# A mixture-of-experts stage whose small products stand in one block for two experts, with TensorE's order fixed to that of the weight loads

## The chip, the cores and the metric

The kernel runs on 1 core of one Trainium2 chip. The metric is the device time of one execution in microseconds, the median of several runs; times of one profiled execution are read from its trace. Engines are PE (TensorE), DVE (VectorE), ACT (ScalarE), POOL (GpSimd) and SP (SyncE), whose queue starts the loads of weights.

## What is computed

A first block of attention, a bidirectional state-space mixer and MLPs on 256 tokens of 1024 numbers is followed by a second block of two layers; each has a token mixer and a mixture of 32 experts. All weights and activations are fp32. Cut to what matters:

```python
for l in range(2):
    mod = silu(c) @ ada_w[l] + ada_b[l]
    sh1, sc1, gt1, sh2, sc2, gt2 = split(mod, 6)
    h = modulate(rms_norm(x, norm1_g[l]), sh1, sc1)
    x = x + gt1 * token_mixer(h, ...)
    h = modulate(rms_norm(x, norm2_g[l]), sh2, sc2)
    x = x + gt2 * hier_moe(h, ...)
return rms_norm(x, final_g)

# hier_moe: the best of 4 groups, then 2 of its 8 experts for a token
hid = silu(xb @ w1[e]) * (xb @ w3[e])      # xb: the tokens of expert e; w1, w3: 1024 x 512
y   = (hid @ w2[e]) * weight               # w2: 512 x 1024; summed over the token's experts
```

## The kernel before

Every expert's 6 MB of weights are loaded whatever the routing. `moe_layer` gives each expert 64 slots and takes the experts in 16 pairs `n`; four experts share a group `G` of gathered tokens. These are its steps:

- `gather(G, d, d + 1)` (L1687) picks the tokens of four experts for 128 of the 1024 numbers: four products with the one-hot tile `OH`, one PSUM tile `pb` (two buffers), one eviction to `XT`. Eight of them make a group. `slot_weights` (L1668) and `oht` (L1679) are eight tiny products and four transposes for a group.
- `up(e, half)` (L1706) multiplies expert `e`'s 64 slots with half of w1 and w3: 8 products for w1 (`o` = 0, output partitions 0 to 63) and 8 for w3 (`o` = 1, partitions 64 to 127) in both halves together, each 64x512, into one PSUM tile `acc` (four buffers). After the second half ACT evicts it as `H` (L1722).
- `act(e)` (L1724) transposes `H` in four products into a `pb` tile and forms silu(a) * b as `aT`.
- `down(n, half)` (L1736) multiplies both experts of a pair (`o` = 0 and 1) with w2: 16 products 64x512 for both halves. `gains` evicts the result, weighted and split in two, as `Y`.
- `scatter(G, t, c)` (L1778) adds the results of four experts to the tokens: four products with `OHT`; four calls make a group. `last` (L1788) does it for the last four experts, straight into the layer's end.
- `general` (L1877) is a branch for a routing in which an expert has more tokens than slots. It is not taken here, but each engine reads a number and jumps over it (L1883).

**Loads.** The class `Stream` cuts the weights into jobs of 1 MB, in the order in which `up` and `down` want them: `up(2n)`, `down(n - 1)`, `up(2n + 1)`; 192 jobs a layer, 4 for an `up` and 4 for the `down` of a pair. A job goes into one of 5 tiles `raw` or one of 7 pairs of half tiles `pre`, a ring of 12 MB. SP's queue (L91) issues a load once the products that read the tile's last contents are done. Before a stage of experts begins, 17 jobs are on their way: 12 in the ring and 5 in tiles that are otherwise free at that time.

**Order on PE.** The code is compiled by a scheduler that reorders instructions within an engine by its own costs, unless `tc.issue_after(i)` says that what is written under it comes behind instruction `i`; this sets an order, it is no wait. Before, `slot_weights`, `gather`, `scatter`, `oht` and `add_x` are appended to a list, and `unit()` takes one step from that list after every two `kk` of `up` and every `f` of `down`. PE's order is otherwise free:

```python
            def unit():
                if todo:
                    todo.pop(0)()
```

Of the kernel before, what the change touches and what calls it, by code (L numbers as in the profile page):

```python
# [1580 lines left out]
def moe_layer(K, l):  # L1581
    nc, tc, I, ws = K.nc, K.tc, K.I, K.ws
    with ExitStack() as ctx:
# [67 lines left out]
        with tc.tile_pool(name="moef", bufs=1, reuse_waits="tile") as q:  # L1651
# [15 lines left out]
            def slot_weights(G):  # L1667

                P = K.pb([128, 2, 2])
                for j in range(2):  # L1670
                    for t in range(2):
                        oh = f32(XT[G][0])[:, t, 2 * j:2 * j + 2].rearrange("p e s -> p (e s)")
                        nc.tensor.matmul(P[:, j], oh, W[:, t, 4 * G + 2 * j:4 * G + 2 * j + 2], start=(t == 0), stop=(t == 1))
                for o in range(2):
                    ps = slice(64 * o, 64 * o + 64)
                    nc.scalar.activation(wcol[ps, 2 * G:2 * G + 2], P[ps, :, o], AF.Copy)

            def oht(G):
                OHT[G] = qr[0].tile([128, 2, 256], FR, name="OHT", tag="OHT", bufs=1)  # L1679
                PT = K.pb([128, 2, 2, 128])  # L1680
                for j in range(2):
                    for t in range(2):
                        oh = f32(XT[G][0])[:, t, 2 * j:2 * j + 2].rearrange("p e s -> p (e s)")
                        nc.tensor.transpose(PT[:, j, t], oh, K.ident)
                nc.scalar.activation(OHT[G], PT.rearrange("p j t l -> p j (t l)"), AF.Copy)

            def gather(G, d0, d1):  # L1687
                OH, xt = XT[G]
                for d in range(d0, d1):
                    P = K.pb([128, 4, 64])  # L1690
                    ds = slice(d * 128, d * 128 + 128)
                    for i, (h, t) in enumerate(((h2h, 0), (h2h, 1), (h2l, 0), (h2l, 1))):
                        nc.tensor.matmul(P.rearrange("p e s -> p (e s)"), h[:, t, ds], OH[:, t].rearrange("p e s -> p (e s)"),  # L1693
                                         start=(i == 0), stop=(i == 3))
# [6 lines left out]
            def unit():  # L1701
                if todo:
                    todo.pop(0)()

            def up(e, half):

                G, i = divmod(e, 4)
                if half == 0:
                    H[e] = K.acc()
                P = H[e]  # L1710
                hs = ws.get(4)
                for u in range(2):
                    for kk in range(2):
                        k = half * 4 + u * 2 + kk
                        for o in range(2):
                            nc.tensor.matmul(P[64 * o:64 * o + 64], XT[G][1][k][:, i], hs[2 * o + u].raw[:, kk],  # L1716
                                             start=(k == 0), stop=(k == 7))
                    unit()
                ws.done(4)
                if half:  # L1720
                    H[e] = q.tile([128, 512], F32, name="H", tag="H", bufs=3)
                    nc.scalar.activation(H[e], P, AF.Copy)  # L1722

            def act(e):  # L1724
                PT = K.pb([128, 4, 2, 64])
                for f in range(4):
                    nc.tensor.transpose(PT[:, f].rearrange("p o s -> p (o s)"), H[e][:, f * 128:f * 128 + 128], K.ident)  # L1727
                del H[e]
                s = q.tile([128, 4, 64], F32, name="s1", tag="s1", bufs=2)
                i = nc.scalar.activation(s, PT[:, :, 0], AF.Silu)  # L1730
                aT[e] = q.tile([128, 4, 64], F32, name="aT", tag="aT", bufs=4)
                j = nc.vector.tensor_tensor(aT[e], s, PT[:, :, 1], OP.mult)  # L1732
                K.ah = i.ins, j.ins

            def down(n, half):
# [4 lines left out]
                for u in range(2):  # L1740
                    f = half * 2 + u
                    for c in range(2):
                        cs = slice(c * 512, c * 512 + 512)
                        for o in range(2):
                            nc.tensor.matmul(PY[c][64 * o:64 * o + 64], aT[2 * n + o][:, f], hs[2 * o + u].raw[:, 0, cs],  # L1745
                                             start=(f == 0), stop=(f == 3))
                    unit()
                ws.done(4)

            def gains(j):  # L1750
# [22 lines left out]
            def scatter_pair(P, j, t, c, start, stop):  # L1773
                ts, cs = slice(t * 128, t * 128 + 128), slice(c * 512, c * 512 + 512)
                for i, y in enumerate(Y[j]):
                    nc.tensor.matmul(P, OHT[j // 2][:, j % 2, ts], y[:, cs], start=start and i == 0, stop=stop and i == 1)

            def scatter(G, t, c):  # L1778
                cs = slice(c * 512, c * 512 + 512)
# [37 lines left out]
            slot_weights(0)  # L1817
            for n in range(16):
                G, i = divmod(n, 2)
                if i == 0 and G:  # L1820
                    later(slot_weights, G)
                if i == 1 and G < 7:
                    later(gather_prep, G + 1)
                    for d in range(8):
                        later(gather, G + 1, d, d + 1)
                if n == 15:
                    for t in range(2):
                        for c in range(2):
                            later(add_x, t, c, out[t][:, c * 512:c * 512 + 512])
                up(2 * n, 0)  # L1830
                if n:
                    act(2 * n - 1)
                up(2 * n, 1)
                if n:
                    down(n - 1, 0)
                    act(2 * n)
                    down(n - 1, 1)
                    if n == 1:
                        K.actx.close()
                        qr.append(rctx.enter_context(tc.tile_pool(name="moer", bufs=1, side="right", reuse_waits="tile")))  # L1840
                        out += K.tail(F32)
                        later(oht, 0)
                    gains(n - 1)
                if i == 0 and G:
                    for t in range(2):
                        for c in range(2):
                            later(scatter, G - 1, t, c)
                    later(oht, G)
# [194 lines left out]
```

## Time and profile before

| what | value |
|---|---|
| median of 3 runs | 2383.11 us (2380.67 to 2383.85) |
| the profiled execution | 2389.19 us |
| its span in the trace | 2387.4 us |
| PE busy | 2300.0 us, 96% of the span |
| PE weight loads busy | 1517.0 us, 64% |
| DVE, ACT busy | 1180.8 us (49%), 812.9 us (34%) |
| q1, the queue of the loads | 663.56 MB, its packets took 76.9% of 16 engines' span |
| L1716, products of `up` | 384.1 us from `raw`, 258.3 us from `pre` |
| L1745, products of `down` | 297.5 us from `pre` |

Busy times of products overlap where two run side by side in PE, so they don't add up to a stage's length. The experts' stages of the two layers lie at about 1065 to 1592 us and 1865 to 2376 us of the span. PE is called busy while a product is under way, whatever part of the array it uses.

### The profile page before, as it was taken

To read this page: it belongs to the slowest core of one execution; us is meant where nothing else is said; L and a number is where in the kernel's file an instruction comes from. 1 tells how busy PE (TensorE), PEld (TensorE's weight loads), DVE (VectorE), ACT (ScalarE), POOL (GpSimd) and SP (SyncE) were. 2 spreads that over 40 slices of the span, in tenths; PEclk is the share of its full clock that TensorE was granted. 3 is DMA by queue.
4 is the path that set the end of the run, shared out by engine and by line. 5 is a ranking of instruction groups with operands and counts; after the bars stand their busy time and mean duration, and the time that the engine had idled before them with its cause. 6 is when DMAs were issued, how large, how long until landed. Compare 5 with 4: busy or idle time off the path is not lost. (4 is left out here: it accounts for less than half of the span.)

```text
span 2387.4 us, 30410 instructions
## 1 busy us (share of the span) xinstructions
PE 2300.0 (96%) x11877; PEld 1517.0 (64%) x11877; DVE 1180.8 (49%) x2024; ACT 812.9 (34%) x1404; POOL 118.7 (5%) x98
## 2 busy tenths in 40 slices
PE   8999999999999999989999999989999999999998
PEld 7878899987888887873333333348887433333333
DVE  6589879996998756651111111236665211111113
ACT  5534446764444444431111111125443111111111
POOL 0000002221000000110000000000011000000000
PEclk9999999998999999989999999999999899999999
DMA  9379854434897544677999999975566799999996
GB/s 330 103 262 360 295 169 136 124 133 159 293 353 260 201 159 140 237 260 291 330 392 389 389 394 394 394 275 190 159 218 220 299 347 361 386 384 393 392 393 245
DMA packets 307104, 669.10 MB, mean 280 GB/s; under 512 B 20996, under 2 KB 60780, under 8 KB 306952
## 3 DMA queue, kind: packets, MB, share of 16 engines
q1 hardware_dynamic: 299496, 663.56, 76.9%
q10 hardware_dynamic: 7456, 3.49, 0.6%
q8 instruction: 97, 1.59, 0.3%
q14 instruction: 55, 0.45, 0.1%
HBM read 665.90 MB, written 1.10 MB: 279 GB/s over the span
## 5 line engine op out<-in xcount | busy, mean ns | idle before, releaser
L162 DVE TENSOR_TENSOR lo<-raw,hi 128x1024 fp32r<-128x1024 f32 (+2 forms) x353 | 433.6, 1237 | 185.4 <-ACT hi L160 184.1
L160 ACT ACTIVATE hi<-raw 128x1024 fp32r<-128x1024 f32 (+2 forms) x353 | 369.5, 1055 | 338.4 <-PE acc L268 227.0
L1716 PE MATMUL acc<-raw,XT 128*64 128x512 f32 x1248 | 384.1, 601 | 0.0
L1745 PE MATMUL pb<-pre,aT 128*64 128x512 f32 x928 | 297.5, 600 | 0.0
L1716 PE MATMUL acc<-pre,XT 128*64 128x512 f32 x784 | 258.3, 598 | 0.0
L266 PE MATMUL acc<-hi,xTh 128*128 128x512 f32 (+2 forms) x608 | 230.3, 381 | 5.5 <-ACT xTh L371 2.9
L267 PE MATMUL acc<-lo,xTh 128*128 128x512 f32 (+2 forms) x608 | 227.6, 375 | 0.0
L268 PE MATMUL acc<-hi,xTl 128*128 128x512 f32 (+2 forms) x608 | 226.5, 377 | 0.1
L1732 DVE TENSOR_TENSOR aT<-s,pb 128x256 f32<-128x256 f32 x64 | 26.9, 421 | 390.2 <-ACT s L1730 390.2
L1716 PEld LDWEIGHTS acc<-raw,XT 128*64 128x64 f32 x1248 | 107.3, 137 | 152.5 <-issue 149.1
L1745 PEld LDWEIGHTS pb<-pre,aT 128*64 128x64 f32 x928 | 86.1, 136 | 136.1 <-issue 126.0
L1722 ACT ACTIVATE H<-acc 128x512 f32<-128x512 f32 x64 | 38.2, 597 | 333.0 <-PE acc L1716 255.8
L1716 PEld LDWEIGHTS acc<-pre,XT 128*64 128x64 f32 x784 | 73.7, 137 | 114.6 <-issue 111.9
L1699 DVE COPY XT<-pb 128x256 f32<-128x256 f32 x64 | 27.2, 425 | 216.5 <-PE pb L1693 216.5
L339 PE MATMUL acc<-xTh,hi 128*128 128x256 f32 x456 | 130.9, 287 | 2.9 <-DVE ca L895 2.9
L266 PEld LDWEIGHTS acc<-hi,xTh 128*128 128x128 f32 x608 | 116.2, 192 | 27.2 <-ACT xTh L371 4.6
L340 PE MATMUL acc<-xTl,hi 128*128 128x256 f32 x456 | 130.1, 285 | 0.0
L341 PE MATMUL acc<-xTh,lo 128*128 128x256 f32 x456 | 129.3, 284 | 0.0
L267 PEld LDWEIGHTS acc<-lo,xTh 128*128 128x128 f32 x608 | 116.2, 191 | 19.7 <-DVE lo L162 0.8
L268 PEld LDWEIGHTS acc<-hi,xTl 128*128 128x128 f32 x608 | 115.4, 191 | 20.1 <-DVE xTl L372 1.0
L339 PE MATMUL pb<-xTh,hi 128*128 128x256 f32 x448 | 126.8, 285 | 1.4 <-ACT hi L160 1.4
L422 POOL TENSOR_TENSOR rstd<-rstd,mhalf 128x1 f32<-128x1 f32 (+2 forms) x36 | 30.4, 847 | 1944.1 <-DVE rstd L421 1899.7
(489 smaller groups left out, 4026.6 us busy)
## 6 DMA issues: line engine op xcount, KB each, us to landing
pre<-in_exp_w SPq DMA_DIRECT2D x428, 512.0 KB
raw<-in_exp_w SPq DMA_DIRECT2D x160, 1024.0 KB
raw<-in_mlp_w SPq DMA_DIRECT2D x64, 1024.0 KB
adaw<-in_ada_w SPq DMA_DIRECT2D x96, 512.0 KB
raw<-in_w_in SPq DMA_DIRECT2D x24, 1024.0 KB
raw<-in_gate_w SPq DMA_DIRECT2D x24, 1024.0 KB
raw<-in_ssm_w_in SPq DMA_DIRECT2D x16, 1024.0 KB
raw<-in_branch_w SPq DMA_DIRECT2D x12, 1024.0 KB
```

Of the source, the lines that this page charges most:

```text
L160: nc.scalar.activation(hi[:, :size], flat, AF.Copy)
L162: eng.tensor_tensor(lo[:, :size], flat, f32(hi[:, :size]), OP.subtract)
L266: nc.tensor.matmul(P, ah, bh, start=start, stop=False)
L267: nc.tensor.matmul(P, ah, bl, start=False, stop=False)
L268: nc.tensor.matmul(P, al, bh, start=False, stop=stop)
L339: nc.tensor.matmul(P, wh, xh[:, k + kk], start=first and start and kk == 0, stop=False, skip_group_check=True)
L340: nc.tensor.matmul(P, wh, xl[:, k + kk], start=False, stop=False, skip_group_check=True)
L341: nc.tensor.matmul(P, wl, xh[:, k + kk], start=False, stop=stop and kk == n - 1, skip_group_check=True)
L422: self.pow = nc.gpsimd.tensor_tensor(r[:, :n], r[:, :n], self.mhalf[:, :n], OP.pow).ins
L1716: nc.tensor.matmul(P[64 * o:64 * o + 64], XT[G][1][k][:, i], hs[2 * o + u].raw[:, kk], start=(k == 0), stop=(k == 7))
L1722: nc.scalar.activation(H[e], P, AF.Copy)
L1745: nc.tensor.matmul(PY[c][64 * o:64 * o + 64], aT[2 * n + o][:, f], hs[2 * o + u].raw[:, 0, cs], start=(f == 0), stop=(f == 3))
```

## The change

The list `todo` and `unit()` are gone. A new function `small(n)` writes all products without expert weights of a pair in one place, between the two halves of `up(2n)`: `act` of both experts of the pair before, and for even `n` the slot weights and the eight gather tiles of the next group, for odd `n` the four scatter calls and `oht` (pair 1, with nothing to scatter yet, has the slot weights of group 0 and the gather tiles of group 1). Each call of `up`, `down` and of what `small` calls goes through `then`, which puts it behind the last product written (`K.pe`), so that PE runs them as written, which is the order of the loads. The PSUM tile of `act` comes from `acc` in place of `pb`, except for the last two experts. `act(30)` moves from the middle of `down(14)` to behind `general`, beside `act(31)`.

```diff
             def act(e):
-                PT = K.pb([128, 4, 2, 64])
+                PT = (K.pb([128, 512]) if e >= 30 else K.acc()).rearrange("p (f o s) -> p f o s", f=4, o=2)
...
-            todo = []
-
...
-            later = lambda f, *a: todo.append(lambda: f(*a))
-
+            def then(f, *a):
+
+                with tc.issue_after(K.pe) if K.pe else nullcontext():
+                    f(*a)
+
+            def small(n):
+
+                G, i = divmod(n, 2)
+                if n:
+                    then(act, 2 * n - 2)
+                    then(act, 2 * n - 1)
+                if i == 0:
+                    if G:
+                        then(slot_weights, G)
+                    if G == 1:
+                        then(oht, 0)
+                    if 0 < G < 7:
+                        then(gather, G + 1, 0, 8)
+                else:
+                    if G == 0:
+                        then(slot_weights, 0)
+                        then(gather, 1, 0, 8)
+                    else:
+                        for t in range(2):
+                            for c in range(2):
+                                then(scatter, G - 1, t, c)
+                        then(oht, G)
...
+            K.pe = None
             prep = gather_prep(0)
             gather(0, 0, 8)
...
             for n in range(16):
...
-                up(2 * n, 0)
-                if n:
-                    act(2 * n - 1)
-                up(2 * n, 1)
+                if n < 14 and n % 2 == 0:
+                    gather_prep(n // 2 + 1)
+                then(up, 2 * n, 0)
+                small(n)
+                then(up, 2 * n, 1)
                 if n:
-                    down(n - 1, 0)
-                    act(2 * n)
-                    down(n - 1, 1)
+                    then(down, n - 1, 0)
+                    then(down, n - 1, 1)
...
-                up(2 * n + 1, 0)
-                if not n:
-                    act(0)
+                then(up, 2 * n + 1, 0)
                 if n == 15 and l == 0:
                     K.norm_rows(1, 0)
-                up(2 * n + 1, 1)
+                then(up, 2 * n + 1, 1)
             gctx.close()
             with tc.tile_pool(name="moeg", bufs=1, reuse_waits="tile") as qg:
                 general(K, qg, l, W, SV, most, h2h, h2l, g2)
+            act(30)
             act(31)
```

In the middle of the first layer's stage, in a pair with scatter products, PE had these in a row before (L1745 is `down`, with `pre` the weights; L1727 is `act`, L1776 the scatter):

```order
L1716 MATMUL acc_12392<-pre_12263,XT_12370 64x512
L1716 MATMUL acc_12392<-pre_12267,XT_12370 64x512
L1745 MATMUL pb2_12439<-pre_12296,aT_12311 64x512
L1745 MATMUL pb2_12440<-pre_12296,aT_12311 64x512
L1727 MATMUL pb_12457<-call_74,H_12437 128x128 x4
L1776 MATMUL pb_12493<-Yh_12343,OHT_12213 128x512
L1776 MATMUL pb_12493<-Yl_12344,OHT_12213 128x512
L1745 MATMUL pb2_12439<-pre_12300,aT_12419 64x512
L1745 MATMUL pb2_12440<-pre_12300,aT_12419 64x512
L1745 MATMUL pb2_12439<-pre_12297,aT_12311 64x512
```

and has these now, right behind the first half of an `up` (L1722 is `act`, L1770 the scatter):

```order
L1712 MATMUL acc_12567<-raw_12395,XT_12117 64x512
L1712 MATMUL acc_12567<-raw_12397,XT_12117 64x512
L1722 MATMUL acc_12580<-call_74,H_12496 128x128 x4
L1722 MATMUL acc_12589<-call_74,H_12565 128x128 x4
L1770 MATMUL pb_12598<-Yh_12348,OHT_12289 128x512
L1770 MATMUL pb_12598<-Yl_12349,OHT_12289 128x512
L1770 MATMUL pb_12598<-Yh_12532,OHT_12289 128x512
L1770 MATMUL pb_12598<-Yl_12533,OHT_12289 128x512
```

The transposes of two experts and all scatter products stand together, and `down`'s products follow one another undisturbed elsewhere.

On SP, the first loads that are issued in the first layer's stage of experts, behind the 17 jobs that are ahead, were these before:

```order
L91 DMA pre_10522<-in_exp_w1_2 128x2x512
L91 DMA pre_10543<-in_exp_w3_2 128x2x512
L91 DMA pre_10547<-in_exp_w2_2 128x1024
L91 DMA raw_10493<-in_exp_w3_2 128x4x512
L91 DMA raw_10495<-in_exp_w1_2 128x4x512
L91 DMA raw_10505<-in_exp_w3_2 128x4x512
L91 DMA pre_10523<-in_exp_w1_2 128x2x512
L91 DMA pre_10544<-in_exp_w3_2 128x2x512
```

and are these now:

```order
L91 DMA raw_10489<-in_exp_w3_2 128x4x512
L91 DMA raw_10491<-in_exp_w1_2 128x4x512
L91 DMA raw_10501<-in_exp_w3_2 128x4x512
L91 DMA raw_10503<-in_exp_w1_2 128x4x512
L91 DMA pre_10518<-in_exp_w1_2 128x2x512
L91 DMA raw_10516<-in_exp_w3_2 128x4x512
L91 DMA pre_10519<-in_exp_w1_2 128x2x512
L91 DMA pre_10530<-in_exp_w3_2 128x2x512
```

Both begin with what PE is done with first: before, tiles of several experts become free in turn, halves of pairs among them; now the tiles of `up(0)` and `up(1)` come first, whole and in their order.

On PE behind the branch of the first layer, before (L1727 is `act(31)`, L1797 `last(14)`):

```order
L1883 UNCONDITIONAL_BRANCH
L1727 MATMUL pb_13293<-call_74,H_12992 128x128 x4
L1797 MATMUL acc_13312<-Yh_12957,OHT_12879 128x512
L1797 MATMUL acc_13312<-Yl_12958,OHT_12879 128x512
L1797 MATMUL acc_13313<-Yh_12957,OHT_12879 128x512
L1797 MATMUL acc_13313<-Yl_12958,OHT_12879 128x512
```

and now (L1722 is `act(30)` and `act(31)`, L1791 `last(14)`):

```order
L1887 UNCONDITIONAL_BRANCH
L1722 MATMUL pb_13284<-call_74,H_12927 128x128 x4
L1722 MATMUL pb_13293<-call_74,H_12983 128x128 x4
L1791 MATMUL acc_13312<-Yh_12948,OHT_12896 128x512
L1791 MATMUL acc_13312<-Yl_12949,OHT_12896 128x512
L1791 MATMUL acc_13313<-Yh_12948,OHT_12896 128x512
L1791 MATMUL acc_13313<-Yl_12949,OHT_12896 128x512
```

The transposes of expert 30 have moved behind the branch.

## Rows read from the trace of the kernel before

**Rows 1.** Table by stretches: us, each engine's busy us (x), PEclk, DMA share, GB/s.

```profile
1200.00:1560.00 360.00, 347.56 (x1505) 138.78 (x1502) 58.36 (x105) 51.50 (x107) 0.00 (x0) 1.00 1.04 392
```

**Rows 2.** Timeline of ACT: start, us, engine line op tile, [idle before <-releaser].

```profile
1263.30 0.60 ACT L1722 ACTIVATE H<-acc 128x512 f32<-128x512 f32 x1 [6.18 <-PE acc L1716]
...
1327.35 0.60 ACT L1722 ACTIVATE H<-acc 128x512 f32<-128x512 f32 x1 [6.18 <-PE acc L1716]
```

**Rows 3.** Waits of the loads' queue, 1260 to 1560: us in total, times, longest.

```profile
SPq L91 <- PE acc L1716: 120.9, 88, 5.8
SPq L91 <- PE pb L1745: 43.9, 35, 2.6
```

**Rows 4.** Waits of PE's weight loads, same stretch.

```profile
PEld pb L1745 <- DMA pre<-in_exp_w: 1.2, 5, 0.2
```

**Rows 5.** Table by stretches, two slices of one load each.

```profile
1397.00:1399.00 2.00, 2.00 (x12) 0.71 (x10) 0.00 (x0) 0.00 (x0) 0.00 (x0) 1.00 1.06 388
1415.00:1417.00 2.00, 2.00 (x10) 0.69 (x6) 0.00 (x0) 0.00 (x0) 0.00 (x0) 1.00 1.02 408
```

**Rows 6.** Table by stretches, front of the first experts' stage.

```profile
1075.00:1090.00 15.00, 15.00 (x63) 5.67 (x63) 1.57 (x6) 0.77 (x2) 0.00 (x0) 0.92 0.22 79
```

**Rows 7.** Timeline of PE, front of the first experts' stage.

```profile
1075.36 1.98 PE L1716 MATMUL acc<-raw,XT 128*64 128x512 f32 x4
```

**Rows 8.** Timeline of the loads' queue, first new load of either stage.

```profile
1085.12 1.24 SPq L91 DMA_DIRECT2D pre<-in_exp_w  x2
...
1877.11 1.24 SPq L91 DMA_DIRECT2D pre<-in_exp_w  x2
```

**Rows 9.** Table by stretches, where the last weights land.

```profile
1570.00:1571.00 1.00, 1.00 (x7) 0.33 (x4) 0.00 (x0) 0.00 (x0) 0.00 (x0) 1.00 0.39 160
2361.00:2362.00 1.00, 1.00 (x8) 0.38 (x5) 0.00 (x0) 0.00 (x0) 0.00 (x0) 1.00 0.53 213
```

**Rows 10.** Timeline of PE, ends of the two experts' stages.

```profile
1581.87 0.40 PE L1797 MATMUL acc<-Yh,OHT 128*128 128x512 f32 x1 [3.83 <-issue]
...
1591.59 1.12 PE L1799 MATMUL acc<-Yl,OHT 128*128 128x512 f32 x2
...
2375.63 0.70 PE L1799 MATMUL acc<-Yl,OHT 128*128 128x512 f32 x1
```

**Rows 11.** Timeline of ACT, end of the second experts' stage.

```profile
2365.34 0.60 ACT L1722 ACTIVATE H<-acc 128x512 f32<-128x512 f32 x1 [5.45 <-PE pb L1745]
```

**Rows 12.** Timeline of PE, single small products between products with weights.

```profile
1503.57 1.93 PE L1745 MATMUL pb<-pre,aT 128*64 128x512 f32 x4
1505.43 0.51 PE L1693 MATMUL pb<-OH,h2h 128*128 128x256 f32 x2
...
1506.10 1.07 PE L1745 MATMUL pb<-pre,aT 128*64 128x512 f32 x2
```

**Rows 13.** Timeline of PE, products with weights alone.

```profile
1586.72 0.59 PE L1745 MATMUL pb<-raw,aT 128*64 128x512 f32 x1
1586.77 0.59 PE L1745 MATMUL pb<-pre,aT 128*64 128x512 f32 x1
1587.15 0.59 PE L1745 MATMUL pb<-raw,aT 128*64 128x512 f32 x1
```

**Rows 14.** Timeline of PE, scatter products.

```profile
1476.38 0.39 PE L1776 MATMUL pb<-Yh,OHT 128*128 128x512 f32 x1
1476.61 0.40 PE L1776 MATMUL pb<-Yl,OHT 128*128 128x512 f32 x1
```

**Rows 15.** Table by stretches: pauses of PE, and the clock.

```profile
1060.00:1070.00 10.00, 6.90 (x34) 6.76 (x33) 4.60 (x21) 3.08 (x4) 2.34 (x1) 0.50 1.05 402
1290.00:1300.00 10.00, 8.85 (x49) 3.91 (x46) 0.85 (x2) 1.75 (x4) 0.00 (x0) 1.00 1.04 391
1575.00:1580.00 5.00, 1.58 (x8) 1.25 (x9) 0.42 (x1) 2.12 (x3) 0.00 (x0) 1.00 0.98 345
1583.00:1584.00 1.00, 1.00 (x4) 0.32 (x5) 0.00 (x0) 0.00 (x0) 0.00 (x0) 0.50 0.05 16
```

More of the change, by code (lines that the diff above doesn't have):

```diff
@@ L1692, in gather @@
                     for i, (h, t) in enumerate(((h2h, 0), (h2h, 1), (h2l, 0), (h2l, 1))):
[L1693 to L1694 removed]
+                        K.pe = nc.tensor.matmul(P.rearrange("p e s -> p (e s)"), h[:, t, ds], OH[:, t].rearrange("p e s -> p (e s)"),
+                                                start=(i == 0), stop=(i == 3)).ins
                     xt[d] = qx.tile([128, 4, 64], F32, name="XT", tag="XT", bufs=16)
@@ L1715, in up @@
                         for o in range(2):
-                            nc.tensor.matmul(P[64 * o:64 * o + 64], XT[G][1][k][:, i], hs[2 * o + u].raw[:, kk],
-                                             start=(k == 0), stop=(k == 7))
-                    unit()
+                            K.pe = nc.tensor.matmul(P[64 * o:64 * o + 64], XT[G][1][k][:, i], hs[2 * o + u].raw[:, kk],
+                                                    start=(k == 0), stop=(k == 7)).ins
                 ws.done(4)
@@ L1744, in down @@
                         for o in range(2):
-                            nc.tensor.matmul(PY[c][64 * o:64 * o + 64], aT[2 * n + o][:, f], hs[2 * o + u].raw[:, 0, cs],
-                                             start=(f == 0), stop=(f == 3))
-                    unit()
+                            K.pe = nc.tensor.matmul(PY[c][64 * o:64 * o + 64], aT[2 * n + o][:, f], hs[2 * o + u].raw[:, 0, cs],
+                                                    start=(f == 0), stop=(f == 3)).ins
                 ws.done(4)
@@ L1775, in scatter_pair @@
                 for i, y in enumerate(Y[j]):
-                    nc.tensor.matmul(P, OHT[j // 2][:, j % 2, ts], y[:, cs], start=start and i == 0, stop=stop and i == 1)
+                    K.pe = nc.tensor.matmul(P, OHT[j // 2][:, j % 2, ts], y[:, cs], start=start and i == 0, stop=stop and i == 1).ins
             def scatter(G, t, c):
@@ L1808, in add_x @@
                 return nc.vector.tensor_tensor(K.x[:, t, cs], K.x[:, t, cs], y, OP.add).ins
-            later = lambda f, *a: todo.append(lambda: f(*a))
+            def then(f, *a):
[22 more added lines that the diff above has]
+                        then(oht, G)
+                    if n == 15:
+                        for t in range(2):
+                            for c in range(2):
+                                add_x(t, c, out[t][:, c * 512:c * 512 + 512])
+            K.pe = None
             prep = gather_prep(0)
@@ L1816, in moe_layer @@
             g2 = K.row(K.mod[l][5:6])
-            slot_weights(0)
             for n in range(16):
[L1819 to L1829, printed above, removed]
-                up(2 * n, 0)
-                if n:
-                    act(2 * n - 1)
-                up(2 * n, 1)
-                if n:
-                    down(n - 1, 0)
-                    act(2 * n)
-                    down(n - 1, 1)
+                if n < 14 and n % 2 == 0:
[3 more added lines that the diff above has]
+                then(up, 2 * n, 1)
+                if n:
+                    then(down, n - 1, 0)
+                    then(down, n - 1, 1)
                     if n == 1:
@@ L1841, in moe_layer @@
                         out += K.tail(F32)
-                        later(oht, 0)
                     gains(n - 1)
[L1844 to L1848, printed above, removed]
-                up(2 * n + 1, 0)
-                if not n:
-                    act(0)
+                then(up, 2 * n + 1, 0)
                 if n == 15 and l == 0:
                     K.norm_rows(1, 0)
-                up(2 * n + 1, 1)
+                then(up, 2 * n + 1, 1)
             gctx.close()
```

9 lines of the change are left out of this document (3 added, 6 removed).

## The prediction

> **What bounds the kernel now.** I read the table by stretches first. In 360 us of the first experts' stage PE is busy 347.56 us, and the DMA engines are at a share of 1.04 with 392 GB/s [rows 1]: two resources look full at once, so the question is which one sets the pace. The timeline of ScalarE gives the period: the eviction of the last `up` of every fourth expert comes 64.05 us after the one before [rows 2], which is 32.03 us for a pair of experts. The waits of the queue that starts the loads say that in 300 us it stood 120.9 us for a product of L1716 and 43.9 us for one of L1745 to free a tile [rows 3]; the other way round PE waited for a load for 1.2 us in all [rows 4]. So PE leads and the loads follow. But they follow closely. A load of w1 or w3 runs at 388 GB/s and one of w2 at 408 [rows 5]. A pair needs 8 MB of the first and 4 of the second: 8 x 1.0486/0.388 + 4 x 1.0486/0.408 = 21.6 + 10.3 = 31.9 us. Taking work off PE therefore buys 0.1 us a pair in the middle of a stage; whatever the change gives has to come where loads have gaps, and those lie at the ends.
>
> At the front the loads stand idle: 79 GB/s in 1075 to 1090 [rows 6]. PE's first product with an expert's weights starts at 1075.36 [rows 7], yet the first new load is issued at 1085.12, in the second layer at 1877.11 [rows 8]: with 12 ring tiles full, nothing can be issued until the breadth-first order of before has finished with one. From 79 GB/s over 15 us (1.19 MB, 3 us at the full rate) bytes flow from 1087.0; about 1.9 us after the issue, so from 1879.0 in the second layer. The last weights land where the rate runs out, at 1570.4 (160 GB/s in the slice) and 2361.6 (213) [rows 9]. Between lie 483.4 and 482.6 us for the 175 of 192 loads that were not there ahead (115 of w1 and w3, 60 of w2); at the rates above they need 310.8 + 154.2 = 465.0 us. So **18.4 and 17.6 us** of a stage are gaps in the loads; some 2.7 and 1.4 us of these I give to other loads in the same queue (an estimate: one row tile of 1 MB or half of it).
>
> **What a tail costs now.** After the last landing PE still runs until `last(15)` starts: 1591.59, 21.2 us after it, in the first layer; 2375.63, 14.0 us after it, in the second [rows 10]. In the second, `up(31)` ends 3.6 us after the landing (its eviction starts at 2365.34 [rows 11]) and the chain from there, through the branch, `act(31)`, `last(14)` and `down(15)`, takes 10.3 us. In the first it takes 17.3, because PE stands 3.83 us with nothing to wait for inside `last(14)` [rows 10], right behind the branch, and goes on at half the clock.
>
> **The change, part by part.** *Products gathered into blocks.* An expert's products have a tile of 128x64, and those of the two halves (`o` = 0 and 1) run side by side. Before, with single small products dropped between them, four records of one half alone took from 1503.57 to 1505.43, 1.86 us, and a lone `gather` tile then 0.67 until 1506.10 [rows 12]. Undisturbed, two records overlap and each half takes its next one 0.43 us later [rows 13]; a pair has 48 products, each of two records, 24 for each half, so 48 x 0.43 = 20.6 us. The scatter products cost 0.23 each [rows 14]. For two pairs I sum 2 x 20.6 = 41.2 for the weights, 8 x 0.67 = 5.4 for the gather, 16 x 0.23 = 3.7 for the scatter, and for 16 transposes of `act`, 4 of `oht` and 8 tiny products at most 0.23 each, between 0 and 6.4, taken as 3.2 in the middle: 53.5, so **26.7 us a pair** (25.1 to 28.4). That is 5.2 us less than the loads' 31.9. PE stops being the bound and waits for weights.
>
> *PE's order is that of the loads.* At the front all 8 gathers come first (5 more than before, 3.4 us), then `up(0)` on its own, whose first two tiles are free after 8 steps of 0.43, 3.4 us: 1075.36 + 6.8 = 1082.2 at full clock, 3 us before 1085.12; at half the clock nothing is won. I take 1.5 us earlier. Then I walk the ring: a step of four products eats 1 MB in 1.72 us, a load brings one in 2.66, the block of pair 1 frees nothing for some 7 us, and the five loads that lie in other tiles free no ring tile either. With these the loads run out of free tiles once after the spare ones (about 3 us), once in `up(3)` (0.7) and once in pair 2's block (4.3): 8 us of gaps remain, 3 to 12 as the block is shorter or longer. Later, PE's slack keeps all tiles in flight. So the last weights land earlier by 18.4 - 2.7 - 8 + 1.5 = **9.2 us** in the first layer and 17.6 - 1.4 - 8 + 1.5 = **9.7** in the second. If the rate that counts is the 392 of a whole stretch [rows 1], the need is 468.1 and each gain 3.1 less.
>
> *The tail.* With PE at the heels of the loads, `up(31)`'s last weights land 4 MB of w2 before the end, 4 x 1.0486/0.408 = 10.3 us, and its last half takes 3.4: it ends 6.9 us before the last landing instead of 3.6 behind it. `act(30)` now stands behind the branch too; its four transposes, hidden before, are on the path for 0.4 at most 0.9. The chain after `up(31)` is then 10.7 in the second layer and 17.7 in the first: it ends 3.8 and 10.8 us behind the landing, a gain of 10.2 and 10.4. But now w2 is in flight at the branch of the second layer too, which is what the first layer's branch has, with its 3.83 us. No row shows that case; the nearest is the first layer's, so I charge the second layer the same chain, and its tail gains 14.0 - 10.8 = **3.2**. The other bound, no such pause, is 10.2. The first layer's **10.4** stands. *PSUM from the four-tile pool* for `act`, and `oht` and `slot_weights` at other places, cost PE at most a microsecond a layer of waiting for an eviction, under the 5.2 of slack; without that slack it would be on the path.
>
> The sum: 9.2 + 9.7 + 10.4 + 3.2 = 32.5 us. The profiled execution took 2389.19, with a span of 2387.4; it would take 2357. The median shown is 2383.11, 6.1 us below that execution, so against it 2351.
>
> **Rivals.** *Slower: the clock.* PE will pause in every half, up to 5.3 us of loads less 3.4 of products, 1.9 us. The trace has stretches where a PE with pauses got half its clock: 6.90 of 10 us busy at 0.50 in 1060 to 1070, and 0.50 in 1583 to 1584 after the 3.83 us pause; against it, 1.00 with 1.58 of 5 us busy in 1575 to 1580, and 1.00 at 8.85 of 10 in the middle of this stage [rows 15]. If a share s of PE's work ran at half the clock, a pair would take 26.7(1 + s). This costs nothing until 31.9 is passed, and eats the gain (32.5 us over 28 pairs, 1.2 each) at s = 0.24; at 0.30 a pair takes 34.7, 28 x 2.8 = 78 more, and the time is 2351 + 78 = 2429. The Trainium skill ("TensorE: Matmul & The Clock Gate", section "HAM oscillation — how this bites in real kernels") says that waits for loads between bursts of products put TensorE back to its lower clock again and again. [...] Chance 0.07.
>
> *A smaller gain.* The pauses behind the branch grow with the loads still running, or the gaps at the front stay at 12: 2 x 5.5 at the front and 5 at the ends leave 16, 2367 (2356 to 2378). For it speaks that the trace has the pause once only, with no releaser that would bound it. 0.15.
>
> *A larger gain.* With PE never holding a tile back, loads could all run at the best rate seen, 408: 175 x 1.0486/0.408 = 449.8, 15 us less a layer, 2321. Against it, the share is already above 1 in both slices of [rows 5]. The Trainium skill ("DMA: Bandwidth & Descriptors", section "Specifications") gives 435 GB/s as the fabric's ceiling, which no row here reaches; by it the loads would need 421.8. 0.07.
>
> *No change.* If the gaps are not PE's doing but the queue's, the loads end when they did and the tail follows the last weights: within 4.8 us of 2383, which is the 0.2% that a measurement of this kernel can tell from no change. 0.05.
>
> **How the numbers follow.** The forecast above has 0.66, its own range 2339 to 2362: with the second tail unpaused 7 less and a 3 us gap at the front 5 less each, with the 392 rate 6 more and long blocks 4 more. The likeliest time is 2351. A range of 2328 to 2370 leaves out the slow clock (0.07), no change (0.05), most of the larger gain (0.04) and the weak end of the smaller one (0.04). Faster by over 0.2%: 0.66 + 0.15 + 0.07 = 0.88; same 0.05; slower 0.07.
>
> **What would show it.** In the profile after: PE's busy time in 1200 to 1560 well under 347, with waits of L1712 and L1740 for loads of some 4 to 5 us a pair, and a granted clock of 1.00; the loading queue waiting for loads, hardly for PE; the same 392 GB/s; the first new load near 1083.5; the last landings some 9 us earlier and `up(31)` ending ahead of them; four pieces, 9 + 10 + 10 + 3. A clock under 0.9 in the stage, a rate other than 392, or a pause longer than 4 us behind a branch would prove a step wrong.

## The result, and the profile after

The changed kernel takes 2347.78 us (median of 4 runs, 2345.05 to 2350.36) against 2383.48 us of the kernel before (4 runs beside them, 2380.67 to 2386.71): a ratio of 0.985 [0.9833, 0.9867], 35.7 us less. The profiled execution took 2345.05 with a span of 2343.3. Of the page, the engines' busy time:

```profile
PE 2198.4 (94%) x11877; PEld 1510.0 (64%) x11877; DVE 1180.4 (50%) x2024; ACT 811.4 (35%) x1404; POOL 118.7 (5%) x98
```

PE is busy 102 us less, although it does the same products. The table by stretches of the changed kernel (columns as in [rows 1]):

```profile
1077.00:1137.00 60.00, 58.65 (x308) 26.78 (x306) 8.66 (x18) 12.55 (x27) 0.00 (x0) 1.00 1.00 360
1137.00:1197.00 60.00, 60.00 (x298) 25.77 (x296) 9.82 (x18) 9.75 (x20) 0.00 (x0) 1.00 1.04 394
1200.00:1500.00 300.00, 269.06 (x1255) 119.82 (x1254) 44.38 (x82) 41.25 (x88) 0.00 (x0) 0.99 1.04 394
1550.00:1556.00 6.00, 3.21 (x13) 2.65 (x14) 0.84 (x2) 0.77 (x2) 0.00 (x0) 0.55 1.04 384
1849.20:1909.20 60.00, 58.65 (x310) 26.84 (x308) 8.67 (x18) 12.56 (x27) 0.00 (x0) 1.00 0.97 362
2321.00:2327.00 6.00, 6.00 (x32) 3.12 (x32) 0.84 (x2) 0.77 (x2) 0.00 (x0) 1.00 0.18 70
2322.00:2323.00 1.00, 1.00 (x6) 0.82 (x5) 0.55 (x2) 0.11 (x1) 0.00 (x0) 1.00 0.40 164
2323.00:2324.00 1.00, 1.00 (x7) 0.36 (x7) 0.00 (x0) 0.00 (x0) 0.00 (x0) 1.00 0.04 16
```

In the middle of a stage the loads run at 394 GB/s, as in [rows 1] within half a per cent, while PE is now idle for 31 of 300 us, and its clock stays at 0.99. ACT's timeline shows the period, and the ends of `up(31)` in both layers:

```profile
1272.70 0.60 ACT L1717 ACTIVATE H<-acc 128x512 f32<-128x512 f32 x1 [3.02 <-PE acc L1712]
...
1336.48 0.60 ACT L1717 ACTIVATE H<-acc 128x512 f32<-128x512 f32 x1 [3.02 <-PE acc L1712]
...
1546.71 0.60 ACT L1717 ACTIVATE H<-acc 128x512 f32<-128x512 f32 x1 [8.04 <-PE acc L1712]
...
2317.42 0.60 ACT L1717 ACTIVATE H<-acc 128x512 f32<-128x512 f32 x1 [8.13 <-PE acc L1712]
```

From 1272.70 to 1336.48 are 63.78 us for two pairs, 31.9 a pair, where [rows 2] had 32.03. What ends PE's waits, in 240 us of this stretch:

```profile
PEld acc L1712 <- DMA raw<-in_exp_w: 42.6, 22, 2.5
```

and the queue of the loads in the same stretch:

```profile
SPq L91 <- DMA pre<-in_exp_w: 59.6, 66, 2.1
SPq L91 <- PE pb L1740: 39.1, 21, 4.2
SPq L91 <- PE acc L1712: 26.7, 23, 2.5
SPq L91 <- DMA raw<-in_exp_w: 17.7, 11, 2.3
```

Against [rows 3] and [rows 4], which cover 300 us, the roles have moved: PE now waits 42.6 us for weights, and SP waits 77.3 us for its own loads to have moved on and 65.8 us for products. Products still free tiles, but the rate of the loads no longer suffers from it.

For the sum the executions have to be cut into stages, because the two profiled ones differ by 7.7 us already before the first expert: the first gather stands at 1072.27 in the kernel before and at 1064.59 in the changed one, and the profiles of the changed kernel's variants below have it anywhere from 1064 to 1072. PE's timeline of the kernel before, first gather of each layer:

```profile
1072.27 0.98 PE L1693 MATMUL pb<-OH,h2h 128*128 128x256 f32 x3 [0.87 <-DVE OH L1663]
...
1864.37 0.98 PE L1693 MATMUL pb<-OH,h2h 128*128 128x256 f32 x3 [0.87 <-DVE OH L1663]
```

and of the changed kernel, first gather, the products behind the branch, and `last(15)` (L1793) of each layer:

```profile
1064.59 0.98 PE L1693 MATMUL pb<-OH,h2h 128*128 128x256 f32 x3 [0.87 <-DVE OH L1663]
...
1550.06 1.45 PE L1722 MATMUL pb<-call,H 128*128 128x128 f32 x8 [3.44 <-PEq L1887]
...
1555.52 0.59 PE L1791 MATMUL acc<-Yl,OHT 128*128 128x512 f32 x1 [2.74 <-issue]
...
1567.23 3.27 PE L1793 MATMUL acc<-Yl,OHT 128*128 128x512 f32 x7 [0.83 <-DVE Yl L1755]
...
1837.23 0.98 PE L1693 MATMUL pb<-OH,h2h 128*128 128x256 f32 x3 [0.87 <-DVE OH L1663]
...
2320.57 1.06 PE L1722 MATMUL pb<-call,H 128*128 128x128 f32 x8 [3.25 <-PEq L1887]
...
2331.39 3.70 PE L1793 MATMUL acc<-Yl,OHT 128*128 128x512 f32 x8 [0.83 <-DVE Yl L1755]
```

From the first gather to `last(15)` the first layer took 519.3 us before (to 1591.59, [rows 10]) and 502.6 now; the second 511.3 (to 2375.63) and 494.2 now. That is 16.7 + 17.1 = **33.8 us**; another 7.7 us of the difference between the two profiled executions lie ahead of the experts and 2.8 between the stages.

### The profile page after: what moved, and what is told of

Same layout as the page of the kernel before. It is cut to its first block, busy times and chain, and to the rows that moved or that the text cites. A ratio compares the mean times of both kernels' runs of the same rounds, so it can differ in the third digit from the quotient of the medians.

```text
span 2343.3 us, 30480 instructions
## 1 busy us (share of the span) xinstructions
PE 2198.4 (94%) x11877; PEld 1510.0 (64%) x11877; DVE 1180.4 (50%) x2024; ACT 811.4 (35%) x1404; POOL 118.7 (5%) x98
## 5 line engine op out<-in xcount | busy, mean ns | idle before, releaser
L1712 PE MATMUL acc<-raw,XT 128*64 128x512 f32 x1248 | 366.5, 603 | 76.0 <-DMA raw<-in_exp_w 75.9
L1712 PE MATMUL acc<-pre,XT 128*64 128x512 f32 x784 | 231.8, 597 | 0.0
L1727 DVE TENSOR_TENSOR aT<-s,acc 128x256 f32<-128x256 f32 x60 | 25.1, 422 | 410.3 <-ACT s L1725 409.8
L1740 PE MATMUL pb<-pre,aT 128*64 128x512 f32 x928 | 208.7, 594 | 0.0
L1764 DVE SCALAR_TENSOR_TENSOR Yl<-pb,wcol,Yh 128x512 fp32r<-128x512 f32 x56 | 40.2, 748 | 296.9 <-ACT Yh L1763 296.0
L1740 PEld LDWEIGHTS pb<-pre,aT 128*64 128x64 f32 x928 | 80.3, 137 | 123.3 <-issue 115.3
L266 PEld LDWEIGHTS acc<-hi,xTh 128*128 128x128 f32 x608 | 115.5, 190 | 26.7 <-ACT xTh L371 4.1
L340 PE MATMUL pb<-xTl,hi 128*128 128x256 f32 x448 | 126.7, 283 | 0.0
```

Of the source, the lines that this page charges most:

```text
L266: nc.tensor.matmul(P, ah, bh, start=start, stop=False)
L340: nc.tensor.matmul(P, wh, xl[:, k + kk], start=False, stop=False, skip_group_check=True)
L1712: K.pe = nc.tensor.matmul(P[64 * o:64 * o + 64], XT[G][1][k][:, i], hs[2 * o + u].raw[:, kk], start=(k == 0), stop=(k == 7)).ins
L1740: K.pe = nc.tensor.matmul(PY[c][64 * o:64 * o + 64], aT[2 * n + o][:, f], hs[2 * o + u].raw[:, 0, cs], start=(f == 0), stop=(f == 3)).ins
L1764: nc.vector.scalar_tensor_tensor(Y[j][1][:, cs], PY[c], wcol[:, j:j + 1], f32(Y[j][0])[:, cs], op0=OP.mult, op1=OP.subtract)
```

## Experiments

All are timed against the kernel before on the same chip; "stages" are the two lengths from the first gather to `last(15)`, read from PE's timeline as above, each of one execution; those of the kernel without the branch come from its second run.

| kernel | median us | ratio to before, interval | stages us |
|---|---|---|---|
| the change | 2347.78 | 0.985 [0.9833, 0.9867] | 502.6, 494.2 |
| the change, again | 2351.71 | 0.9852 [0.9828, 0.9875] | 500.8, 496.0 |
| order only | 2350.86 | 0.9865 [0.9844, 0.9886] | 500.4, 495.4 |
| blocks only | 2360.45 | 0.9898 [0.9877, 0.9919] | 504.5, 498.5 |
| 16 products more | 2359.82 | 0.9898 [0.9877, 0.9919] | 500.9, 503.0 |
| 32 products more | 2434.51 | 1.0213 [1.0192, 1.0233] | not read |
| gather split | 2348.99 | 0.9857 [0.9835, 0.9879] | 501.4, 495.1 |
| act(30) back | 2352.95 | 0.9884 [0.9862, 0.9906] | 502.6, 498.0 |
| no branch | 2334.28 | 0.9793 [0.9772, 0.9813] | 490.7, 491.2 |
| branch ahead of pair 14 | 2345.84 | 0.9846 [0.9823, 0.9869] | 496.0, 494.9 |
| branch in the last pair | 2340.01 | 0.981 [0.979, 0.9829] | 493.3, 492.0 |
| w2 first | 2360.87 | 0.9894 [0.9869, 0.9918] | 505.6, 502.8 |

**Order without blocks.** The list of single steps is back; every pair of `kk` or `f`, every step and every `act` goes through `then`. `act` has its PSUM tile from `pb` again, and `act(30)` stands inside `down(14)`.

```diff
+                    then(two)
+                    unit()
...
+            def unit():
+                if todo:
+                    then(todo.pop(0))
```

> The order on TensorE is fixed to that of the loads, but the small products stay single, one step behind every four weight products, and act(30) stays inside down(14). My theory: what the change won is that the products of both halves run side by side in order and the tiles come free in order; a single small product costs then only a switch of some 0.2 us, 9 of them a pair make 26.7 + 1.8 = 28.5 us a pair, still under the 31.9 of the loads. So 2344 to 2356 us, ratio 0.984 to 0.988, as with blocks. Rival: the blocks are what counts, single products keep TensorE at 32 us a pair: 2378 to 2388.

2350.86 us, as my theory had it. The blocks are not what brings the time: with single steps PE is still fast enough, though with less to spare, since it waits 16.8 us for weights in the stretch where the change waits 42.6:

```profile
PEld acc L1713 <- DMA raw<-in_exp_w: 16.8, 9, 3.0
```

**Blocks without order.**

```diff
-                with tc.issue_after(K.pe) if K.pe else nullcontext():
-                    f(*a)
+                f(*a)
```

> The blocks are written as in the change, but the order is left to the scheduler, which spreads the gather tiles among weight products again. My theory: the middle of a stage stays bound by the loads at 392 GB/s, the tails gain as in the change (14 us), and the gain at the front (19 us of load gaps) is lost in good part since tiles come free late again: 2358 to 2372 us. Rival 1, the text's blocks are enough: 2344 to 2354. Rival 2, without the fixed order nothing is left: 2378 to 2388.

2360.45 us, inside the first range. A part of the loss against the change is at the front, as expected: 341 GB/s in the 60 us that begin 12.4 us behind the first gather, where the change has 360 from the same point on, 3 us; then both run at 394.

```profile
1082.00:1142.00 60.00, 60.00 (x280) 25.12 (x279) 6.83 (x15) 10.50 (x23) 0.00 (x0) 1.00 0.92 341
1142.00:1202.00 60.00, 60.00 (x285) 25.46 (x280) 10.06 (x19) 9.66 (x21) 0.00 (x0) 1.00 1.04 394
```

But most of the gain is there without a fixed order, 27.6 of 33.8 us by the stages, which I had not expected so clearly. Whichever half of the change is made, PE falls below the loads: with blocks alone it catches up at 29.9 us a pair behind the front (ACT's evictions from 1256.66 to 1376.32, four pairs), where the loads need 31.9.

**More work for PE.** `idle` is called in the block of pairs 1 to 15 and puts 16 or 32 products into a PSUM tile that nobody reads.

```diff
+            def idle():
+                P = K.pb([128, 512])
+                for i in range(16):
+                    K.pe = nc.tensor.matmul(P, h2h[:, 0, 0:128], h2h[:, 1, 0:512], start=(i == 0), stop=(i == 15)).ins
```

> The changed kernel with 16 products of 128x512 more in each of 30 blocks, whose result nobody reads: 16 x 0.23 = 3.7 us more for TensorE a pair, 110 us in all. My theory, loads bound the stages and TensorE has some 5 us of slack a pair: only the longer block at the front costs something, 2346 to 2358 us. Rival, TensorE still sets the pace: 2348 + 110 = 2450 to 2465.

> The same with 32 products, 7.4 us a block, 221 us in all: 26.7 + 7.4 = 34.1 us a pair, over the loads' 31.9. My theory: 30 x 2.2 = 66 us are paid and the rest is hidden, 2405 to 2430 us, the rate of the loads in 1200 to 1500 falls to 392 x 31.9/34.1 = 367 GB/s. Rival, TensorE sets the pace already: 2560 to 2575. Second rival, the slack is 7 us or more: under 2370.

With 16, 110 us more work cost 8 to 12 us against the two medians of the change, 2 us beyond my range. In the middle of a stage it is hidden, as the first of these two rows shows (16 products more, then 32); what is paid lies at the front, where the first 60 us of loads run at 327 and 317 GB/s in the two layers instead of 360 and 362. PE's idle time alone, 31 of 300 us or 3.3 a pair in the change, would have shown less slack than the 3.7 us a pair that cost nothing here.

```profile
1200.00:1500.00 300.00, 297.84 (x1438) 147.28 (x1435) 45.48 (x83) 42.94 (x89) 0.00 (x0) 1.00 1.04 394
1200.00:1500.00 300.00, 300.00 (x1471) 155.11 (x1470) 42.44 (x78) 40.97 (x86) 0.00 (x0) 1.00 0.99 368
```

With 32 it is 2434.51, 4 us above my range: PE sets the pace there, busy throughout, with the loads at 368 GB/s. Its period gives PE's own time, free of waits for loads but for the 4.1 us that PE's weight loads wait in these 300:

```profile
1277.72 0.60 ACT L1717 ACTIVATE H<-acc 128x512 f32<-128x512 f32 x1 [3.94 <-PE acc L1712]
...
1345.92 0.60 ACT L1717 ACTIVATE H<-acc 128x512 f32<-128x512 f32 x1 [3.94 <-PE acc L1712]
```

and the block of 32 products by itself:

```profile
1295.59 7.53 PE L1810 MATMUL pb<-h2h 128*128 128x512 f32 x32
1302.96 0.40 PE L1770 MATMUL pb<-Yh,OHT 128*128 128x512 f32 x1
```

68.20 us for two pairs are 34.1 a pair; less the 7.37 from 1295.59 to 1302.96, 26.7 us are left, the sum of the prediction.

**The first load earlier.**

```diff
-            gather(0, 0, 8)
+            gather(0, 0, 4)
...
                 then(up, 2 * n, 0)
+                if not n:
+                    then(gather, 0, 4, 8)
```

> The changed kernel with only four gather tiles of group 0 ahead of up(0, 0) and four behind it. My theory: the first tiles come free, and the first new load goes out, some 2.4 us earlier in each stage, and since the loads set the pace all of it is kept, less what later gaps of the ring swallow: 2342 to 2347 us. Rival: the ring runs out of free tiles later anyway, so nothing is won: 2346 to 2350.

The rival was right: 2348.99. The first load is issued 7.5 us behind the first gather (1066.12) instead of 10.2, as SP's timeline shows,

```profile
1073.65 6.92 SPq L91 DMA_DIRECT2D raw<-in_exp_w  x4
```

but the first 60 us of loading then run at 349 GB/s, where the change has 360:

```profile
1076.00:1136.00 60.00, 58.66 (x309) 26.89 (x310) 7.59 (x17) 11.50 (x27) 0.00 (x0) 1.00 0.96 349
```

A load that starts earlier only reaches the ring's next shortage earlier. 1.7 of the 2.7 us are given back there, and the rest does not show in the stages: 501.4 us in the first layer, where the two executions of the change have 502.6 and 500.8, and 495.1 in the second for 494.2 and 496.0.

**act(30) at its old place**, between the halves of `down(14)`.

```diff
                     then(down, n - 1, 0)
+                    if n == 15:
+                        then(act, 30)
                     then(down, n - 1, 1)
...
-            act(30)
             act(31)
```

> The changed kernel with act(30) back between the halves of down(14), where TensorE has slack. My theory: its four transposes leave the path behind the branch, 0.3 to 0.5 us a layer, within the noise of the time (2344 to 2350) but to be seen in the timeline: four products instead of eight before last(14), and the chain from up(31) to last(15) shorter by 0.3 to 0.5 in the second layer. Rival: its eviction or the order holds down(14) up, 2 us or more later.

2352.95, 3 us above my range and above both medians of the change (2347.78 and 2351.71). My theory was wrong: from the eviction of `up(31)` to `last(15)` it takes 22.6 and 18.1 us in the two layers, where the change has 20.5 and 14.0. The rival has the time but not the cause, since `up(31)` is not held up (its eviction stands 479.9 us behind the first gather in the second layer, 480.2 in the change). What is longer is PE's pause at the jump, 5.16 us in the first layer and 4.96 in the second for the change's 3.44 and 3.25, and half the clock follows it in the second layer too (0.50 in 2326 to 2330). The edit also moved four products of `down(15)` ahead of the branch (at 2318.99 and 2319.44). Moving `act(30)` behind the branch was no loss; why the jump takes longer here is not settled.

```profile
2325.85 1.08 PE L1722 MATMUL pb<-call,H 128*128 128x128 f32 x4 [4.96 <-PEq L1888]
```

**The branch.** First it is left out:

```diff
-            with tc.tile_pool(name="moeg", bufs=1, reuse_waits="tile") as qg:
-                general(K, qg, l, W, SV, most, h2h, h2l, g2)
```

> The changed kernel without the branch for crowded experts (leaves out what it would compute for a routing in which an expert has more tokens than slots; this routing has none). My theory: TensorE's pauses behind the branch, 3.44 and 2.74 us in the first layer and 3.25 in the second, come from the jump while weights are still being loaded, and the half clock behind them is their consequence. Without it act starts some 0.8 us after up(31): 2.6 + 2.7 + 3.5 (clock) = 8.9 us in the first layer and 2.5 in the second, 2334 to 2339 us. Rival: the pauses are waits for the loads or for the evictions and stay: 2345 to 2351.

> The kernel without the branch again, for its timeline. My theory: up(31), act, last(14) and down(15) follow each other in both layers with no pause over 1 us and a clock of 1.00, so the chain from the end of up(31) to last(15) is 10 to 11.5 us in both layers instead of 20.6 and 14.1. Rival: the second pause of the first layer, inside last(14), stays.

2334.28 us, and 2333.2 in the second run: 13.5 us less than the change. The timeline of the first layer, `act(31)`, `down(15)` and `last(15)`:

```profile
1547.65 0.66 PE L1722 MATMUL pb<-call,H 128*128 128x128 f32 x4
...
1549.30 2.36 PE L1740 MATMUL pb<-raw,aT 128*64 128x512 f32 x9 [0.52 <-DVE aT L1727]
...
1556.37 1.12 PE L1793 MATMUL acc<-Yl,OHT 128*128 128x512 f32 x2
```

No pause over 0.52 us is left, and the clock stays at 1.00 while 395 GB/s are loaded:

```profile
1546.00:1557.00 11.00, 10.48 (x43) 3.79 (x38) 1.75 (x3) 1.99 (x4) 0.00 (x0) 1.00 1.04 395
```

From the eviction of `up(31)` to `last(15)` it takes 9.5 us in the first layer and 10.3 in the second. So both pauses of the first layer and the half clock behind them hang on the branch. Part of the gain has another source, which I had not named: the branch is a wall for the scheduler, and without it six of the eight products of `last(14)` run in PE's waits for `up(31)`, ahead of the rows shown.

Then it stands ahead of the 15th pair (this needs the gathered tiles in two pools, so that one can be closed earlier):

```diff
+                if n == 14:
+                    ectx.close()
+                    with tc.tile_pool(name="moeg", bufs=1, reuse_waits="tile") as qg:
+                        general(K, qg, l, W, SV, most, h2h, h2l, g2)
...
```

> The changed kernel with the branch ahead of the 15th pair, where TensorE has slack (the gathered tiles of even and odd groups in two pools, one weight buffer less inside the branch, which is not entered here). My theory: the same pauses occur there, in front of up(28), but the slack of 4 to 5 us a pair takes them up before the last loads land; the tails are those of the kernel without the branch: 2334 to 2341 us. Rival: a pause so late in the stage holds the ring back and costs as much as at the end: 2345 to 2352.

2345.84, in the range of the rival; the second stage gained nothing (494.9, where the change has 494.2 and 496.0). But it is not PE's pause that holds the ring back. SP jumps as well, and its waits between 1490 and 1516 show what that costs it:

```profile
SPq L1891 <- SPq L1891: 12.2, 3, 6.3
```

For 12.2 us no load is issued, and the loads run dry:

```profile
1508.00:1511.00 3.00, 0.87 (x3) 0.20 (x4) 0.00 (x0) 0.00 (x0) 0.00 (x0) 1.00 0.18 70
```

So it was moved behind `up(30)` of the last pair, where SP has issued all loads of the layer (`if n == 15`, after `then(up, 2 * n, 1)`):

> The changed kernel with the branch inside the last pair, behind up(30) and half of down(14), where SP has issued all loads of the layer (gathered tiles in two pools and one weight buffer less inside the branch, as in the kernel with the branch ahead of the 15th pair). My theory: SP's own jump now holds no load back, TensorE's pause of 3.2 us lies in front of waits of 0.3 and 1.7 us for up(31)'s weights and delays up(31) by 1.3 us, and the chain behind up(31) has no pause and no half clock: 7.4 us less in the first layer and 1 less in the second, 2336 to 2342 us. Rival: the later pause inside last(14) is not the branch's and stays: 2343 to 2349.

2340.01 us, the fastest whole kernel of this study: 11.7 us under the change beside it. PE's pause is there, 2.68 us in front of `act(30)`, and is swallowed in part: the waits for `up(31)`'s weights that follow in the change, 0.23 and 1.65 us in the first layer, are gone, and `up(31)` ends 1.7 and 2.3 us later than there, seen from the first gather. Behind it no pause is over 0.52 us, and from its eviction to `last(15)` it takes 9.5 us in both layers.

```profile
1541.84 0.63 PE L1724 MATMUL pb<-call,H 128*128 128x128 f32 x4 [2.68 <-PEq L1891]
...
1565.01 1.55 PE L1795 MATMUL acc<-Yl,OHT 128*128 128x512 f32 x3
```

**Loads in flight at the branch.** The job list has `down(15)` ahead of `up(31)`, and the tiles are given back together at the end:

```diff
+        if n == 15:
+            j += down(15)
         j += up(2 * n + 1)
-    return j + down(15)
+    return j
...
```

> The changed kernel with the w2 weights of the last pair loaded ahead of those of up(31), all other work the same, so that in the second layer no load is in flight when TensorE reaches the branch. It ends later by some 6 us a layer, since up(31) now waits for the very last weights. My theory: TensorE's pause at the branch is the fetch of instructions behind the loads in flight; then it is 0.6 to 1.0 us in the second layer instead of 3.25 (it was 0.77 there before the change), 2350 to 2362 us. Rival: the length of the pause comes from where the code stands or from the branch itself: 3 us or more there, 2353 to 2365.

2360.87, which lies in both ranges, so the time decides nothing; the pause does. In the second layer the loads end before PE gets there, and the pause behind the jump is 1.18 us in place of 3.25, near the 0.6 to 1.0 of my theory and far from the rival's 3. In the first layer, where the next layer's weights are being loaded, it is 3.02, but there the trace names DVE's `lo` as what PE waited for last, not the jump.

```profile
1563.72 1.06 PE L1725 MATMUL pb<-call,H 128*128 128x128 f32 x8 [3.02 <-DVE lo L162]
...
2325.46 1.94 PE L1714 MATMUL acc<-raw,XT 128*64 128x512 f32 x2 [8.58 <-DMA raw<-in_exp_w]
...
2339.24 1.09 PE L1725 MATMUL pb<-call,H 128*128 128x128 f32 x8 [1.18 <-ACTq L1896]
```

```profile
2329.00:2332.00 3.00, 3.00 (x10) 0.95 (x8) 0.00 (x0) 0.00 (x0) 0.00 (x0) 0.50 0.67 256
2334.00:2339.00 5.00, 4.06 (x18) 1.12 (x14) 0.00 (x0) 0.60 (x1) 0.00 (x0) 1.00 0.02 7
```

This speaks for the loads as what makes the jump slow, but one row speaks against it. In the first layer of the kernel with 32 products more, loads run at 391 to 405 GB/s from 1592.0 to 1593.5, just before the pause, and it is 0.93 us:

```profile
1594.10 1.09 PE L1722 MATMUL pb<-call,H 128*128 128x128 f32 x8 [0.93 <-ACTq L1893]
```

Those loads had begun only 3 us earlier (nothing moved up to 1590). What exactly is waited for was not measured apart; that code is fetched through the same DMA engines is my reading of the queue q8 "instruction" on the page, no more.

**The changed kernel again**, timed beside the kernel with w2 first and that with the branch in the last pair:

> The changed kernel as it is, beside the others on the same chip: 2345 to 2352 us by any theory.

2351.71 us: the ratio is the same to 0.0002, while the two medians of one and the same kernel differ by 4 us, and those of the kernel before by 7 (2382.09 to 2388.89). Differences under 5 us are therefore read from the stages, not from the medians. This execution also shows that the ends of the stages are not the same each time: in the second layer half the clock followed the pause at the jump, which it did not in the other.

```profile
2326.98 1.07 PE L1722 MATMUL pb<-call,H 128*128 128x128 f32 x8 [3.23 <-PEq L1887]
```

```profile
2327.00:2331.00 4.00, 4.00 (x16) 3.17 (x16) 0.84 (x2) 0.77 (x2) 0.00 (x0) 0.61 0.29 116
```

## Why the prediction was right, step by step

2351 was forecast, 2347.78 measured, in the range and near its middle. The four pieces add up to 32.5 us, the stages of the two profiled executions differ by 33.8. By layers the sum is less good: 19.6 us were forecast for the first and 16.7 came, 12.9 for the second and 17.1 came. That the two errors, 2.9 and 4.2 us in opposite directions, leave 1.3 us is luck.

- *PE at 26.7 us a pair, the loads at 31.9.* Both came out to the digit: 26.7 by the 32 products more, 31.9 by the period. For the first the digit is luck, since the sum took the middle of 25.1 to 28.4. And the reason given, single products dropped among weight products, was only half of it: with single steps in a fixed order PE is fast enough too.
- *The front.* Gaps of 8 us were expected; 360 GB/s instead of 394 over 60 us is 5.2 us, and in the second layer, from the first landing on, 362 over 60 us is 4.9. The first load was to come 1.5 us earlier and came 2.6 earlier, 10.2 us behind the first gather instead of 12.85 (SP's timeline of the change):

```profile
1074.80 4.49 SPq L91 DMA_DIRECT2D raw<-in_exp_w  x4
```

  By the split gather this term was worth next to nothing by itself; the shorter gaps were worth more.
- *The end of `up(31)`.* It was to move by the loads' 9.2 and 9.7 us and by 3.6 + 6.9 for its place ahead of the last w2: 19.7 and 20.2. Seen from the first gather, its eviction (before: the line below in the first layer, [rows 11] in the second) moved from 502.0 to 482.1 and from 501.0 to 480.2: 19.9 and 20.8.

```profile
1574.28 0.60 ACT L1722 ACTIVATE H<-acc 128x512 f32<-128x512 f32 x1 [5.45 <-PE pb L1745]
```

  In the second layer the eviction stands 5.0 us ahead of the last landing, which the 164 GB/s in 2322 to 2323 put at 2322.4, read as the prediction read [rows 9]; 6.9 were expected. The landing itself moved by 12.0 us, from 497.2 to 485.2 behind the first gather; 9.7 were expected. So the total held, and its two terms erred by about 2 us each in opposite directions. In the first layer the next layer's loads follow at once, and the last landing can't be read off the rate.
- *The chain behind it.* Here two errors cancel. 17.7 us were charged in both layers; the first took 20.5 (1546.71 to 1567.23), the second 14.0 (2317.42 to 2331.39). Before, PE's first products behind the branch stood at

```profile
1576.47 0.63 PE L1727 MATMUL pb<-call,H 128*128 128x128 f32 x4 [2.17 <-PEq L1883]
...
2366.13 0.66 PE L1727 MATMUL pb<-call,H 128*128 128x128 f32 x4 [0.77 <-ACTq L1883]
```

  In the first layer the pause at the jump grew from 2.17 to 3.44, but the second one fell from 3.83 to 2.74, so that the two together stayed at 6 us; what is longer is the time at half the clock (0.55 in 1550 to 1556), and a wait of 0.83 for DVE's `Yl` is new in front of `last(15)`. In the second the pause at the jump grew from 0.77 to 3.25, but the second pause, the one that the prediction named, did not come, nor half the clock: 1.00 in 2321 to 2327. I had taken the first layer's chain whole, as the nearest row; what came was between the two bounds, 3.7 us from the one and 3.3 from the other. In the other execution of the change, with half the clock in the second layer too, the chains took 19.5 and 15.5.
- *The rivals.* The clock did not fall in the stage: the granted clock is 0.99 with waits up to 2.5 us. The Trainium skill ("TensorE: Matmul & The Clock Gate", section "HAM oscillation — how this bites in real kernels") tells of a kernel whose waits for loads, longer than the products between them, bring the lower clock back each time. The runs here agree for a long wait, with a granted clock of 0.50 behind 8.58 us in the kernel with w2 first. The waits in the middle of a stage, up to 2.5 us and shorter than the products between them, are not the case that the Trainium skill tells of. The loads got no faster, 394 GB/s, so the larger gain is out. The pause at the branch grew in the second layer, as the smaller gain had it, but the front was better.

## What to carry to other kernels

When two resources look full, work out each one's own time for a period: it tells how much an edit of the one can bring before the other takes over, here 0.1 us a pair in the middle and everything at the ends. Once loads set the pace, look where they run dry (front of the ring, jumps of the engine that issues them) and how much work stands behind the last byte. A branch that is never taken costs each engine that jumps, PE here mostly more with loads in flight, and it keeps the scheduler from filling waits across it: put it where the other engines have slack and no load is left to issue.

## What the runs showed of the hardware that was not expected

A jump over the branch cost PE 0.77, 1.18 and 1.19 us where no loads were in flight (the second layer of the kernel before, of the one with w2 first and of the one with 32 products more). With loads it was 1.63 us (second layer, blocks only) to 5.16 us (first layer, `act(30)` back), with the one exception of 0.93 us shown above. SP's queue stood 12.2 us in three waits at its jump ahead of pair 14 in the first layer, and 10.5 and 14.8 us at the jumps of the change.

The time that passes ahead of the first expert differs from run to run by some 8 us for reasons that no edit here touches (first gather from 1063.79 to 1072.27).

The granted clock fell to half behind waits of 3.44, 4.96 and 8.58 us, but the length of a wait alone does not decide it. The second layer of the change has 1.00 behind 3.25 us in one execution and 0.61 behind 3.23 in the other, the kernel with the order alone 0.56 in 2330 to 2332 behind 3.25, and the first layer of the change's other execution 1.00 in 1554.8 to 1557 behind 3.50. What does decide was not tested.
